# Weight stores on ScalarE's queue, token norms from the transposed input, and attention biases and maxima as product rows

## The chip, the cores and the metric

The kernel runs on one core of a Trainium2 chip. The metric is the device time of one execution in microseconds. Before the change it is 1830.58 us, the median of 3 runs (1828.81 to 1836.41).

## What is computed

One layer of a streaming encoder. 2048 prompt tokens and 128 sample tokens (8 sequences of 16), each 1024 wide, are normalised and projected to the columns of three groups of heads; the gated outputs of the groups go through one output projection.

```python
h = rms_norm(x, norm_g) @ w_in
fox_cols, rwkv_cols, mem_cols = jnp.split(h, [FOX_COLS, FOX_COLS + RWKV_COLS], axis=-1)
q, k, v, logf, g_f = fox_prep(fox_cols, fox_q_g, fox_k_g, fox_b_f)
...
s = s + jnp.transpose(cq, (0, 2, 1))[..., :, None] - jnp.transpose(ck, (0, 2, 1))[..., None, :]
mask = kpos[None, :] <= qpos[:, None]
s = jnp.where(mask, s, jnp.finfo(jnp.float32).min)
p = jax.nn.softmax(s, axis=-1)
...
o = jnp.concatenate([o_f.astype(x.dtype) * jax.nn.silu(g_f),
                     o_r * jax.nn.silu(g_r),
                     o_m * jax.nn.silu(g_m)], axis=-1)
y = x + o @ w_out
```

`fox` is causal attention with 6 heads of 64 whose logits carry a bias: `c`, the running sum of the log forget gates, is added for the query and subtracted for the key. `rwkv` is a recurrent mixer with 6 heads, `mem` is attention with 4 heads over 256 memory tokens. All is in float32.

## The kernel before, in words

**Products in two parts.** A float32 matrix is held as a high part, rounded to the type fp32r, and a low part, the rest. A product is then three fp32r products: high by high, high by low, low by high.

**First part (the pools of `p1`).** The tokens are taken in four passes of 512. The first pass has the 128 sample tokens as well, so 640. `prep_x` (L218 on) prepares a pass: it loads the tokens as rows, squares them on ScalarE with a running sum per row (L238 in the first pass, L243 later), takes the power -1/2 on GpSimd, and turns the factors into a row for all partitions (`pb`, copied to `rb`, L252). It then loads the transposed tokens in 8 tiles of 128 rows (`xraw`, L267), scales them on VectorE (L65 is the helper's line), and splits them into `xk` (high by ScalarE, L270, low by GpSimd or VectorE). In the first pass this is done for 256 columns and then for 384.

`wd_load` (L172 on) brings weights: in the first pass it loads the raw ones (L196), makes the high part on ScalarE (L197) and the low part on GpSimd, and stores both parts in DRAM (`w_d`, L200); the later passes load the stored parts (L192). `proj_d` makes columns by tokens (`pjd`), `wide` tokens by columns (`pjt`). Results of `wide` go through the buffer `qk` (two of them, L705) to DRAM (L713). In the last pass `forget` works out the running sums and stores the negated ones as rows `nc_d`.

**Second part (`p2`).** The fox heads go in 3 pairs by 4 query blocks of 512, the memory heads in 2 pairs by 4 blocks. Keys are loaded per 512 tokens (`tok`, L980), turned by TensorE (`pt`, L983) and split into `K1` and `K2`; queries into `Q1` and `Q2`. `fox_max` makes the scores once with the queries on the partitions (`pm`), adds the key bias (`nb`, a copy of the bias row in all 128 partitions, L1011), and takes the row maximum, both in one VectorE instruction (L1063). `negate` and `rows_` turn the negated maxima to a row: a transpose (`pr`, L1082), a copy to `m8` (L1084), a store to DRAM (L1086) and two loads into row 64 of `Q2` (L1088). `scores` then makes the scores again with the keys on the partitions (`pS`) in two products. The first has the query's high and low parts stacked against the key's high part twice, the second the query's high part with the row of maxima against the key's low part with a row of ones. The exponential (L1117) adds the key's bias per partition and gives `P`, which ScalarE and GpSimd split into `Ph` (L1120) and `Pl`; `values` makes the outputs `po`. The sample tokens' attention (`sample`) and the output projection (`py`, in pieces) are mixed in between.

**What sets the order.** The code emits all instructions, and `_arrange` at its end orders each engine's instructions anew. It simulates the engines and the DMA queue with costs written in `_Op`, several times with other ranks (`_TRIES`, `_AGAIN`), and keeps the order with the least total. Every DMA of the kernel before is issued by SP, so all share one queue, which takes them in order: a transfer that must wait for its data holds those behind it.

Of the kernel before, what the change touches and what calls it, by code (L numbers as in the profile page):

```python
# [9 lines left out]
F32 = mybir.dt.float32  # L10
# [7 lines left out]
KC = 8  # L18
# [33 lines left out]
def kernel(ctx: ExitStack, tc: tile.TileContext, I: dict, O: dict):  # L52
# [62 lines left out]
    nc_d = dt("nc_d", [6, TP])  # L115
# [7 lines left out]
    with ExitStack() as p1:  # L123
# [48 lines left out]
        def wd_load(*parts, src="w_in"):  # L172
# [14 lines left out]
            for j, k0 in enumerate(range(0, KC, 4)):  # L187
# [5 lines left out]
                else:  # L193
# [5 lines left out]
                    if key in split:  # L199
                        SY.dma_start(split[key][128 * j:128 * j + 128], flat.bitcast(F32))  # L200
# [17 lines left out]
        def prep_x(tok0, n, xtok, xT, gcol, tiles=None, between=lambda: None):  # L218
# [9 lines left out]
            for t0, t1 in ((0, 2), (2, 5)) if first else ((0, nt),):  # L228
                c0, c1 = 128 * t0, 128 * t1
                for t in range(t0, t1):  # L230
                    if first:
                        if t % 2 == 0:
                            two = rv.tile([128, 2, D], F32, tag="gm" if t < 4 else "su", name="xt", bufs=2 if t < 4 else 1)
                        xt = two[:, t % 2]
                    r0 = TP if t == 4 else tok0 + 128 * t
                    if first:
                        SY.dma_start(xt, xtok[r0:r0 + 128, :])
                        S.activation(xt, xt, AF.Square, accum_out=ssq[:, 0, t:t + 1])  # L238
                    else:
# [4 lines left out]
                if not first:  # L244
                    tt(V, ssq[:, 0, :nt], ssq[:, 0, :nt], ssq[:, 1, :nt], A_)
                rsqrt_small(rsq[:, t0:t1], ssq[:, 0, t0:t1], t1 - t0, 1.0 / D, EPS)
# [6 lines left out]
                for k in range(KC):  # L253
                    if not t0:
                        xk.append(tiles[k] if tiles else xs_.tile([128, 2, 640], F32R, tag="xk", name="xk", bufs=XKB))
                        if not first:
                            raw = xs_.tile([128, 512], F32, tag="xraw", name="xraw", bufs=3)
                        elif k < 6:
                            if k % 3 == 0:
                                three = ws.tile([128, 2, 4, 256], F32, tag="hl", name="xraw").rearrange("p x a b -> p (x a b)")  # L260
                            raw = three[:, 640 * (k % 3):640 * (k % 3) + 640]
                        else:
                            raw = rv.tile([128, 640], F32, tag=("bk", "bt")[k - 6], name="xraw")
                        raws.append(raw)
                    raw, hl = raws[k], xk[k]
                    for a, m, r0 in spans(tok0, c0, c1 - c0):
                        SY.dma_start(raw[:, c0 + a:c0 + a + m], xT[128 * k:128 * (k + 1), r0:r0 + m])  # L267
# [520 lines left out]
        def forget():  # L788
# [137 lines left out]
    with ExitStack() as p2:  # L926
# [21 lines left out]
        S.copy(negT, negm[:, 2, :])  # L948
        idb = c2t("idb", [128, 128], BF16)
# [20 lines left out]
        def split_keys(k1, k2, src, n):  # L970
            src = src[:, :n]
            S.copy(k1[0:64, :n], src)
            S.copy(k1[64:128, :n], src)  # L973
            tt(V, k2[0:64, :n], src, k1[0:64, :n].bitcast(F32), SUB)
            G.memset(k2[64:65, :n].bitcast(F32), 1.0)
# [20 lines left out]
        def fox_keys(U, hp):  # L996
# [4 lines left out]
            def block(g0):  # L1001
                if not g0:
                    U["nb"] = kp.tile([128, 2, TP], F32, tag="nb", name="nb")
                gs = slice(g0, g0 + 512)
                pt = turned_in(k_d[gs, cs], 512)
                k1 = [kp.tile([128, 512], F32R, tag="K1", name="K1", bufs=2 * NKB) for _ in range(2)]
                k2 = [kp.tile([65, 512], F32R, tag="K2", name="K2", bufs=2 * NKB) for _ in range(2)]
                for h in range(2):
                    split_keys(k1[h], k2[h], pt[64 * h:64 * h + 64], 512)
                for h in range(2):  # L1010
                    SY.dma_start(U["nb"][:, h, gs], nc_d[2 * hp + h, gs].partition_broadcast(128))  # L1011
# [7 lines left out]
        def mem_keys(U, hp):  # L1019
            cs = slice(128 * hp, 128 * hp + 128)  # L1020

            def step():
# [3 lines left out]
                k1 = [m[:, 256 * h:256 * h + 256] for h in range(2)]  # L1026
                k2 = [m[0:65, 512 + 256 * h:768 + 256 * h] for h in range(2)]
# [6 lines left out]
        def queries(U, q, qsrc, qb, hp, fox):  # L1034

            s_ = "" if fox else "m"

            def load():
                pt = turned_in(qsrc, 512)
                if fox:  # L1040
                    q["Q1"] = [wk.tile([128, 512], F32R, tag=f"Q1{h}", name=f"Q1{h}") for h in range(2)]
                    q["Q2"] = [wk.tile([65, 512], F32R, tag=f"Q2{h}", name=f"Q2{h}") for h in range(2)]
                else:
                    m = big("Qm", F32R)
                    q["Q1"] = [m[:, 512 * h:512 * h + 512] for h in range(2)]
                    q["Q2"] = [m[0:65, 512 * h:512 * h + 512] for h in (2, 3)]
# [5 lines left out]
                q["mx"] = wk.tile([128, 2, 4], F32, tag="mx" + s_, name="mx", bufs=1 + fox)  # L1052

            def fox_max(h, t, c0, nk):
# [4 lines left out]
                if end:  # L1059
                    mm(pm[:, n - 128:n], idb, negb, start=False)  # L1060
                jk = wk.tile([128, 512], BF16, tag="jk", name="jk", bufs=1)
                m_ = q["mx"][:, h, t:t + 1]
                V.tensor_tensor_reduce(out=jk[:, :n], in0=pm[:, :n], in1=U["nb"][:, h, c0:c0 + n], scale=1.0,  # L1063
                                       scalar=-3.0e38 if c0 == 0 else m_, op0=A_, op1=MAX, accum_out=m_)
# [947 lines left out]
```

## Time and profile before

| | before |
|---|---|
| median of 3 runs | 1830.58 us (1828.81 to 1836.41) |
| the profiled execution, its own time | 1832.25 us |
| its span | 1830.5 us |
| TensorE busy | 1718.1 us, 94% |
| mean granted clock of TensorE | 0.971 |
| VectorE, ScalarE, GpSimd busy | 934.0, 872.3, 782.4 us |
| DMA | 301.34 MB, mean 165 GB/s |

In the profile PE is TensorE's matmuls and PEld its weight loads, which overlap them; DVE is VectorE, ACT ScalarE, POOL GpSimd, SP SyncE, and SPq its sequencer that issues DMAs. A row of the groups reads: line, engine, operation, output<-inputs, shapes, count | busy us, mean ns of one | idle time of the engine just before them, and what ended most of it. A row of the timeline begins with its start and its length in us, and a bracket gives the idle time before it and what ended that. A row of the waits reads: engine, what waited, what it waited for: us in total, times, the longest. Many lines go through helpers (L59 is every product, L62, L65 and L68 the elementwise ones), so the names tell them apart.

### The profile page before, as it was taken

The numbers are of one execution on the slowest core, as the hardware profiler recorded it, in microseconds if no ns is written. First come the engines' busy times: TensorE is split into PE (matmuls) and PEld (weight loads), VectorE is DVE, ScalarE is ACT, GpSimd is POOL, SyncE is SP. The second block draws the span as 40 slices with busy tenths as digits, with TensorE's granted clock in tenths as the row PEclk, the third lists the DMA queues.
The fourth block names the chain that finished last, engine by engine and source line by source line (L and its number), as shares of the span: only waits on it lengthen the run. The fifth ranks groups of instructions, "written<-read, shape, count | busy, mean of one in ns | idle before, by whom it ended". The sixth has DMA issues, their size and how long they took to land. (4 is left out here: it accounts for less than half of the span.)

```text
span 1830.5 us, 42049 instructions
## 1 busy us (share of the span) xinstructions
PE 1718.1 (94%) x16743; PEld 1370.1 (75%) x16743; DVE 934.0 (51%) x2325; ACT 872.3 (48%) x1727; POOL 782.4 (43%) x790
## 2 busy tenths in 40 slices
PE   4989999999999999999999998799899898999998
PEld 3989989788887788887888886567576555667776
DVE  6543354474444564364754543867346654485213
ACT  5424342533243424325232433687787565986351
POOL 5565252232322243031322241377586364866562
PEclk9999999999999999999999998799999898999999
DMA  7665463644445645456454454434647645262432
GB/s 230 246 219 200 144 205 125 202 163 151 168 157 168 223 128 190 138 174 195 155 170 134 134 177 123 156 121 143 203 138 248 195 141 173 87 209 87 163 111 89
DMA packets 213273, 301.34 MB, mean 165 GB/s; under 512 B 57444, under 2 KB 162454, under 8 KB 197206
## 3 DMA queue, kind: packets, MB, share of 16 engines
q1 hardware_dynamic: 213078, 298.66, 49.6%
q8 instruction: 131, 2.15, 0.5%
q14 instruction: 64, 0.52, 0.1%
HBM read 211.47 MB, written 87.12 MB: 163 GB/s over the span
## 5 line engine op out<-in xcount | busy, mean ns | idle before, releaser
L59 PE MATMUL pjd<-xk,w 128*128 128x512 f32 (+4 forms) x2280 | 520.1, 373 | 14.6 <-DVE xk L62 6.7
L59 PEld LDWEIGHTS pjd<-xk,w 128*128 128x128 f32 (+1 forms) x2280 | 381.9, 190 | 79.1 <-issue 10.8
L62 POOL TENSOR_TENSOR Pl<-P,Ph 128x512 fp32r<-128x512 f32 (+3 forms) x272 | 315.5, 1174 | 150.5 <-ACT Ph L1120 127.6
L59 PE MATMUL pjt<-w,xk 128*128 128x256 f32 x2040 | 292.6, 291 | 4.4 <-ACT qk L705 4.4
L59 PEld LDWEIGHTS pjt<-w,xk 128*128 128x128 f32 x2040 | 263.9, 191 | 17.9 <-issue 7.7
L59 PE MATMUL py<-W,oh 128*128 128x512 f32 x816 | 236.2, 402 | 2.3 <-DVE rb L1162 1.6
L1117 ACT ACTIVATE P<-pS,NB 128x512 f32<-128x512 f32 x240 | 147.9, 623 | 85.6 <-PE pS L59 57.5
L59 PEld LDWEIGHTS py<-W,oh 128*128 128x128 f32 x816 | 150.5, 190 | 38.3 <-DVE rb L1162 2.1
L59 PE MATMUL pS<-Q,K 128*128 128x512 f32 (+2 forms) x480 | 155.5, 392 | 8.3 <-ACT P L1117 8.0
L1120 ACT CAST Ph<-P 128x512 fp32r<-128x512 f32 (+3 forms) x272 | 150.1, 564 | 7.7 <-PE po L59 2.9
L59 PE MATMUL po<-Ph,vt 128*65 128x512 f32 x480 | 151.3, 373 | 1.2 <-ACT ob L1143 0.7
L59 PEld LDWEIGHTS pS<-Q,K 128*128 128x128 f32 (+1 forms) x480 | 87.4, 195 | 40.5 <-ACT P L1117 24.7
L62 DVE TENSOR_TENSOR xo<-py,xo 128x512 f32<-128x512 f32 x68 | 46.5, 686 | 133.1 <-PE py L59 127.8
L59 PE MATMUL pm<-K,Q 128*128 128x512 f32 (+2 forms) x240 | 95.8, 411 | 19.5 <-DVE Q L62 13.1
L62 POOL TENSOR_TENSOR nr<-nr,mhalf 128x8 f32<-128x8 f32 (+2 forms) x43 | 61.2, 1424 | 122.9 <-DVE nr L68 106.4
L1063 DVE CUSTOM_DVE_ANT_0 jk<-pm,nb,mx 128x512 bf16<-128x512 f32 (+3 forms) x144 | 93.2, 647 | 33.7 <-PE pm L59 25.1
L62 POOL TENSOR_TENSOR w<-wraw,w 128x1024 fp32r<-128x1024 f32 (+1 forms) x34 | 79.6, 2343 | 46.6 <-ACT w L197 42.2
L59 PE MATMUL po<-Pl,vt 128*65 128x512 f32 x240 | 88.3, 369 | 1.8 <-POOL Pl L62 1.7
L705 ACT COPY qk<-pjt 128x512 f32<-128x512 f32 (+1 forms) x47 | 26.5, 563 | 131.0 <-PE pjt L59 104.3
L59 PEld LDWEIGHTS po<-Ph,vt 128*65 128x65 f32 x480 | 64.0, 139 | 27.3 <-ACT Ph L1120 2.4
L59 PEld LDWEIGHTS pm<-K,Q 128*128 128x128 f32 x240 | 47.1, 198 | 44.7 <-DVE mx L1063 18.2
L62 POOL TENSOR_TENSOR oh<-ot,oh 128x384 fp32r<-128x384 f32 (+2 forms) x38 | 44.9, 1183 | 74.3 <-ACT oh L1323 39.5
(392 smaller groups left out, 2820.9 us busy)
## 6 DMA issues: line engine op xcount, KB each, us to landing
w<-w_d SPq DMA_DIRECT2D x84, 1024.0 KB
w_d<-w SPq DMA_DIRECT2D x28, 1024.0 KB
y_d<-xo SPq DMA_DIRECT2D x21, 512.0 KB
wraw<-in_w_in SPq DMA_DIRECT2D x36, 256.0 KB
xo<-in_x SPq DMA_DIRECT2D x17, 512.0 KB
xo<-y_d SPq DMA_DIRECT2D x17, 512.0 KB
xt<-in_x SPq DMA_DIRECT2D x24, 256.0 KB
xraw<-in_xT SPq DMA_DIRECT2D x24, 256.0 KB
```

Of the source, the lines that this page charges most:

```text
L59: PE.matmul(out, lhsT, rhs, start=start, stop=stop, skip_group_check=True)
L62: e.tensor_tensor(out=out, in0=a, in1=b, op=op)
L705: S.copy(o_, out)
L1063: V.tensor_tensor_reduce(out=jk[:, :n], in0=pm[:, :n], in1=U["nb"][:, h, c0:c0 + n], scale=1.0, scalar=-3.0e38 if c0 == 0 else m_, op0=A_, ...
L1117: S.activation(P_[:, c0:], pS[:, c0:], AF.Exp, bias=NB[:, qb, 2 * hp + h, kt:kt + 1] if fox else 0.0)
L1120: S.copy(Ph[:, c0:], P_[:, c0:])
```

## The change

It has four parts and a change to the planner.

- The stores of the split weights are issued by ScalarE instead of SP, so they have a queue of their own.
- In the first pass the tokens' row loads go. The transposed tiles are loaded earlier, ScalarE squares them into a scratch tile, and products with a column of ones (`pq`, one column each, 40 in all) sum them over the partitions.
- The key bias of the maxima becomes two rows (high and low part) of `K1`, against rows of ones in `Q1`; the broadcast `nb` and the fused add and maximum go, and a plain maximum per 512 keys stays. `K1` now has 67 rows with the high part, and `K2` has the high part over the low part.
- The row of negated maxima is made by four fp32r products with an identity (`pr`, 33 rows of 128) and two copies of a row into `Q1`; the store and the two loads go.
- The planner charges DMAs to the engine that issues them, with a wire for each queue, and takes six rounds instead of five.

```diff
-nc_d = dt("nc_d", [6, TP])
+nc_d = dt("nc_d", [12, TP])
...
                     if key in split:
-                        SY.dma_start(split[key][128 * j:128 * j + 128], flat.bitcast(F32))
+                        S.dma_start(split[key][128 * j:128 * j + 128], flat.bitcast(F32))
...
+                if first:
+                    m = c1 - c0
+                    sqs = [rv.tile([128, 8, 256], F32, tag="gm", name="xsq", bufs=2)] if not t0 else [
+                        rv.tile([128, 5, 384], F32, tag="gm", name="xsq", bufs=2), rv.tile([128, 3, 384], F32, tag="su", name="xsq2")]
+                    pq = ps.tile([128, 512], F32, tag="ra", name="pq")
+                    for k in range(KC):
...
+                        for a, w, r0 in spans(tok0, c0, m):
+                            SY.dma_start(raws[k][:, c0 + a:c0 + a + w], xT[128 * k:128 * (k + 1), r0:r0 + w])
+                        sq = sqs[k // 5 if t0 else 0][:, k % 5 if t0 else k, :]
+                        S.activation(sq, raws[k][:, c0:c1], AF.Square)
+                        for t in range(t1 - t0):
+                            mm(pq[:, t:t + 1], sq[:, 128 * t:128 * t + 128], one1, start=k + t == 0, stop=k == KC - 1)
+                    rsqrt_small(rsq[:, t0:t1], pq[:, 0:t1 - t0], t1 - t0, 1.0 / D, EPS)
...
-            nr = sm.tile([96, 128], F32, tag="w4", name="nr", bufs=1)
-            V.tensor_copy(nr, pn[0:96, 0:128])
-            SY.dma_start(nc_d.rearrange("h (t p) -> (h t) p", p=128), nr)
+            nr = sm.tile([96, 2, 128], F32R, tag="w4", name="nr", bufs=1)
+            S.copy(nr[:, 0], pn[0:96, 0:128])
+            tt(V, nr[:, 1], pn[0:96, 0:128], nr[:, 0].bitcast(F32), SUB)
+            for a in range(2):
+                SY.dma_start(nc_d[6 * a:6 * a + 6].rearrange("h (t p) -> (h t) p", p=128), nr[:, a].bitcast(F32))
...
             S.copy(k1[0:64, :n], src)
-            S.copy(k1[64:128, :n], src)
-            tt(V, k2[0:64, :n], src, k1[0:64, :n].bitcast(F32), SUB)
-            G.memset(k2[64:65, :n].bitcast(F32), 1.0)
+            S.copy(k2[0:64, :n], src)
+            tt(V, k2[64:128, :n], src, k1[0:64, :n].bitcast(F32), SUB)
+            G.memset(k1[64:65, :n].bitcast(F32), 1.0)
...
-                for h in range(2):
-                    SY.dma_start(U["nb"][:, h, gs], nc_d[2 * hp + h, gs].partition_broadcast(128))
+                    SY.dma_start(k1[h][65:67, :].bitcast(F32), nc_d[2 * hp + h:2 * hp + h + 7:6, gs])
...
-                    S.copy(q["Q2"][h][0:64], src)
-                    tt(V, q["Q1"][h][64:128], src, q["Q1"][h][0:64].bitcast(F32), SUB)
+                    S.copy(q["Q2"][h][64:128], src)
+                    tt(V, q["Q2"][h][0:64], src, q["Q1"][h][0:64].bitcast(F32), SUB)
+                    if fox:
+                        G.memset(q["Q1"][h][64:67].bitcast(F32), 1.0)
...
-                V.tensor_tensor_reduce(out=jk[:, :n], in0=pm[:, :n], in1=U["nb"][:, h, c0:c0 + n], scale=1.0,
-                                       scalar=-3.0e38 if c0 == 0 else m_, op0=A_, op1=MAX, accum_out=m_)
+                V.tensor_reduce(out=q["mx"][:, h, t, c0 // 512:c0 // 512 + 1], in_=pm[:, :n], op=MAX, axis=AX.X)
...
-                PE.transpose(pr[0:8, 0:128], q["mx"].rearrange("p h t -> p (h t)"), ident)
-                m8 = wk.tile([8, 128], F32R, tag="m8", name="m8")
-                S.copy(m8, pr[0:8, 0:128])
-                md = dt("md", [8, 128], bufs=4)
-                SY.dma_start(md, m8.bitcast(F32))
+                for t in range(4):
+                    mm(pr[0:33, 128 * t:128 * t + 128], q["mr"][:, t, :], idr)
                 for h in range(2):
-                    SY.dma_start(q["Q2"][h][64:65, :].bitcast(F32), md[4 * h:4 * h + 4].rearrange("(o t) c -> o (t c)", o=1))
+                    S.copy(q["Q1"][h][64:65], pr[32 * h:32 * h + 1])
...
-                mm(pS[:, c0:], k1, q["Q1"][h][:, c0:], stop=False)
+                mm(pS[:, c0:], k2, q["Q2"][h][:, c0:], stop=False)
                 diag = fox and kt >= 4 * qb
-                mm(pS[:, c0:], k2, q["Q2"][h][:, c0:], start=False, stop=not diag)
+                mm(pS[:, c0:], k1[0:65], q["Q1"][h][0:65, c0:], start=False, stop=not diag)
...
-_AGAIN = 5
+_AGAIN = 6
...
-            rank = [(1 - _SHIFT) * a + _SHIFT * b for a, b in zip(rank, late)]
+            rank = [(1 - _SHIFT) * a + _SHIFT * (b + c) / 2 for a, b, c in zip(rank, start, late)]
```

The order shifts all through the program. Three places matter here. The first is ScalarE at the program's start. There `xt` are the tokens as rows with their sums `ssq`, `xsq` the squares of the transposed tiles, `rb` the row of factors, `xk` the high parts and `w` those of the weights. Before:

```order
L197 CAST w<-wraw 128x280 x2
L238 ACTIVATE xt,ssq<-xt 128x1024 x5
L252 COPY rb<-pb 128x256
L270 CAST xk<-xraw 128x256
L252 COPY rb<-pb 128x256
L270 CAST xk<-xraw 128x256
```

And with the change:

```order
L247 ACTIVATE xsq<-xraw 128x256 x8
L247 ACTIVATE xsq<-xraw 128x384 x3
L265 COPY rb<-pb 128x256
L247 ACTIVATE xsq<-xraw 128x384 x2
L275 CAST xk<-xraw 128x256 x2
L247 ACTIVATE xsq_247<-xraw 128x384
L275 CAST xk<-xraw 128x256 x4
L247 ACTIVATE xsq_247<-xraw 128x384
L197 CAST w<-wraw 128x280 x2
```

The squares of the second half now stand between the copies of the first, and the first weights' high parts come after them.

The second place is ScalarE a little later in the first pass, with the change, where the stores `w_d<-w` stand among the high parts of weights (L197) and the evictions of `pjt` into `qk`:

```order
L710 COPY qk<-pjt 128x512
L692 ACTIVATE nsq<-qk 128x512
L710 COPY qk<-pjt 128x512
L692 ACTIVATE nsq<-qk 128x512
L197 CAST w<-wraw 128x1024 x2
L710 COPY qk<-pjt 128x256
L200 DMA w_d<-w 128x2048 x2
L692 ACTIVATE nsq<-qk 128x256
L197 CAST w<-wraw 128x1024 x2
L710 COPY qk<-pjt 128x512 x2
```

Before, no DMA stands in this engine's row; the stores stood in SP's, between the raw weights and the stores of `qk`.

The third place is SP's queue at the entry into the attention: `tok` and `vtok` are the keys, queries and values of a block, `nb` the broadcast bias, `K` the rows of bias. Before:

```order
L980 DMA tok<-k_d 128x4x128
L988 DMA vtok<-v_d 128x4x128
L980 DMA tok<-q_d 128x4x128
L941 DMA negm<-in_negm 128x384
L1011 DMA nb<-nc_d 128x512 x6
L754 DMA mg_d<-gth 128x512
L1011 DMA nb<-nc_d 128x512
L980 DMA tok<-k_d 128x4x128
L1011 DMA nb<-nc_d 128x512
L647 DMA o_d<-bv 128x512
```

And with the change:

```order
L995 DMA tok<-q_d 128x4x128
L948 DMA negm<-in_negm 128x384
L759 DMA mg_d<-gth 128x512
L930 DMA out_rs_p<-sstp 64x6x64
L652 DMA o_d<-bv 128x512
L1023 DMA K_14040<-nc_d 2x512
L995 DMA tok<-k_d 128x4x128
L1003 DMA vtok<-v_d 128x4x128
L995 DMA tok<-q_d 128x4x128
L1023 DMA K_14041<-nc_d 2x512
```

The second block's keys, values and queries follow the first block's after a handful of rows, without the eight broadcasts ahead of them.

More of the change, by code (lines that the diff above doesn't have):

```diff
@@ L229, in prep_x @@
                 c0, c1 = 128 * t0, 128 * t1
[L230 to L239, printed above, removed]
+                if first:
[4 more added lines that the diff above has]
+                    for k in range(KC):
+                        if not t0:
+                            if k < 6:
+                                if k % 3 == 0:
+                                    three = ws.tile([128, 2, 4, 256], F32, tag="hl", name="xraw").rearrange("p x a b -> p (x a b)")
+                                raws.append(three[:, 640 * (k % 3):640 * (k % 3) + 640])
+                            else:
+                                raws.append(rv.tile([128, 640], F32, tag=("bk", "bt")[k - 6], name="xraw"))
+                        for a, w, r0 in spans(tok0, c0, m):
[5 more added lines that the diff above has]
+                    rsqrt_small(rsq[:, t0:t1], pq[:, 0:t1 - t0], t1 - t0, 1.0 / D, EPS)
+                else:
+                    for t in range(t0, t1):
+                        r0 = tok0 + 128 * t
                         for j in range(2):
@@ L243, in prep_x @@
                             S.activation(xt, xt, AF.Square, accum_out=ssq[:, j, t:t + 1])
-                if not first:
                     tt(V, ssq[:, 0, :nt], ssq[:, 0, :nt], ssq[:, 1, :nt], A_)
-                rsqrt_small(rsq[:, t0:t1], ssq[:, 0, t0:t1], t1 - t0, 1.0 / D, EPS)
+                    rsqrt_small(rsq[:, t0:t1], ssq[:, 0, t0:t1], t1 - t0, 1.0 / D, EPS)
                 pb = pj.tile([128, 512], F32, tag="pj", name="pb")
@@ L256, in prep_x @@
                         if not first:
[L257 to L264, printed above, removed]
+                            raws.append(xs_.tile([128, 512], F32, tag="xraw", name="xraw", bufs=3))
+                            SY.dma_start(raws[k][:, :n], xT[128 * k:128 * (k + 1), tok0:tok0 + n])
                     raw, hl = raws[k], xk[k]
-                    for a, m, r0 in spans(tok0, c0, c1 - c0):
-                        SY.dma_start(raw[:, c0 + a:c0 + a + m], xT[128 * k:128 * (k + 1), r0:r0 + m])
                     for r_, o, a, b in cuts:
@@ L948 @@
         S.copy(negT, negm[:, 2, :])
+        idr = c2t("idr", [128, 128], F32R)
+        S.copy(idr, ident)
+        turnm = [c2t(f"turnm{j}", [128, 4, 33], F32R) for j in range(4)]
+        for x in turnm:
+            G.memset(x.bitcast(F32), 0.0)
+        taken = [0, 0]
         idb = c2t("idb", [128, 128], BF16)
@@ L1025, in step @@
                 pt = turned_in(mk_d[:, cs], 256)
-                k1 = [m[:, 256 * h:256 * h + 256] for h in range(2)]
-                k2 = [m[0:65, 512 + 256 * h:768 + 256 * h] for h in range(2)]
+                k1 = [m[0:65, 256 * h:256 * h + 256] for h in range(2)]
+                k2 = [m[:, 512 + 256 * h:768 + 256 * h] for h in range(2)]
                 for h in range(2):
@@ L1036, in queries @@
             s_ = "" if fox else "m"
+            q["mr"] = turnm[2 * (not fox) + taken[fox] % 2]
+            taken[fox] += 1
             def load():
@@ L1553, in __init__ @@
             return
+        self.wire = 0
         psum = any("PSUM" in space(a) for a in aps)
         scalar = n > 1 and any(k == 1 for k in sizes)
-        if eng == "SP":
+        if "DMA" in kind:
             size = 4 * list(outs[0].ap)[0][1] * _free(list(outs[0].ap))
@@ L1776, in _schedule @@
     ready, end, done, start = [0] * count, [0] * count, [False] * count, [0] * count
-    released, alive, pooled, wire, base, order, why = {}, set(), {}, 0, 0, [], [[] for _ in nodes]
+    released, alive, pooled, wire, base, order, why = {}, set(), {}, {}, 0, [], [[] for _ in nodes]
     cand = {e: [x for x in range(count) if not need[x] and of[x] == e] for e in free}
@@ L1837, in _schedule @@
         c = cost[nodes[x][0]]
-        if e == "SP":
+        if e == "SP" or e == "Activation" and c.wire:
             free[e] = s + c.own
-            wire = max(wire, s + c.own + 300) + c.wire
-            end[x] = wire + c.time
+            a, b = max(wire.get(e, 0), s + c.own + 300), max([0] + [t for q, t in wire.items() if q != e])
+            wire[e] = a + c.wire + min(max(0, b - a), c.wire)
+            end[x] = wire[e] + c.time
         elif e == "PE":
```

38 lines of the change are left out of this document (20 added, 18 removed).

## The prediction

> **What bounds the kernel now.** I read the page first (engine shares, the slices), then the windows, then the timelines of the stretches in which TensorE stands still.
>
> ```profile
> span 1830.5 us, 42049 instructions
> PE 1718.1 (94%) x16743; PEld 1370.1 (75%) x16743; DVE 934.0 (51%) x2325; ACT 872.3 (48%) x1727; POOL 782.4 (43%) x790
> ...
> PE   4989999999999999999999998799899898999998
> ...
> PEclk9999999999999999999999998799999898999999
> ```
>
> TensorE is the bound: busy 1718.1 us, so 112.4 us are idle, and they lie at the start, past the middle (slices 25 and 26) and in the last third. In the same places the granted clock sinks. A change that leaves the products alone can only win back idle time and time at a low clock. Four stretches, with PE busy in the first busy column and the clock in the column before the DMA share:
>
> ```profile
> 0.00:50.00 50.00, 22.96 (x104) 18.60 (x105) 30.79 (x72) 25.98 (x57) 23.51 (x33) 0.90 0.78 243
> 100.00:150.00 50.00, 43.21 (x334) 41.63 (x333) 22.66 (x59) 15.02 (x28) 29.54 (x25) 0.97 0.58 195
> ...
> 1130.00:1200.00 70.00, 53.05 (x234) 35.38 (x232) 52.95 (x124) 45.46 (x89) 23.65 (x27) 0.76 0.54 170
> 1200.00:1700.00 500.00, 467.77 (x2722) 321.38 (x2721) 291.47 (x708) 364.30 (x690) 321.83 (x302) 0.96 0.49 161
> ```
>
> Idle: 27.0, 6.8, 17.0 and 32.2 us, 83 of the 112. Lost to the clock: 5.0, 1.5, 16.8 and 20 us (share missing times length). The change touches all four.
>
> **The start: norms from the transposed tokens.**
>
> ```profile
> 0.74 2.10 SPq L196 DMA_DIRECT2D wraw<-in_w_in  x4
> ...
> 4.65 1.28 ACT L197 ACT_TABLE_LOAD   x1 [4.65 <-DMA wraw<-in_w_in]
> ...
> 9.81 1.06 ACT L238 ACTIVATE xt<-xt 128x1024 f32<-128x1024 f32 x1 [3.12 <-DMA xt<-in_x]
> ...
> 14.93 0.19 ACT L238 ACTIVATION_READ_ACCUMULATOR xt<-xt 128x1 f32 x1
> ...
> 16.16 2.50 PE L59 MATMUL pb<-ident,rsq 128*128 128x128 f32 x10 [16.16 <-POOL rsq L62]
> ...
> 17.83 5.06 DVE L65 SCALAR_TENSOR_TENSOR xraw<-xraw,vec,rb 128x256 f32<-128x256 f32 x9 [2.44 <-ACT rb L252]
> ...
> 18.74 0.41 ACT L270 CAST xk<-xraw 128x256 fp32r<-128x256 f32 x1 [0.95 <-DVE xraw L65]
> ...
> 30.60 0.55 DVE L62 TENSOR_TENSOR xk<-xraw,xk 128x384 fp32r<-128x384 f32 x1
> ...
> 35.30 0.28 DVE L65 SCALAR_TENSOR_TENSOR centre<-bones,ident 128x128 f32<-128x128 f32 x1
> ...
> 36.37 1.05 DVE L62 TENSOR_TENSOR xk<-xraw,xk 128x384 fp32r<-128x384 f32 x1 [0.79 <-ACT xk L270]
> ...
> 41.79 18.48 PE L59 MATMUL pjd<-xk,w 128*128 128x256 f32 x110 [1.89 <-DVE fl L62]
> ```
>
> Before, five loads of 512 KB must land and be squared; scaling starts 2.71 us after the last read-out ends (15.12 to 17.83). Then VectorE scales and splits until 37.42, and full-width products start at 41.79. Now eight loads of 128 KB are first in SP's queue. At 0.525 us an issue (2.10 for 4) the last is issued at 4.9; at the 1.8 us from the weights' last issue (2.84) to their first use after that wait (4.65), it is there at 6.7. The first has landed at 3.1 by the same lag, the table load of 1.28 follows, and ScalarE squares eight tiles of 256 at about 0.41 us (the copy of that size), done near 7.7; the column products add some 0.4 (an estimate from small products elsewhere), so scaling starts near 10.8, 7 us earlier. The second half waits for more: 22 further issues lie ahead of its last load, which lands at 18 to 20; squares, column products and the 2.71 put its scaling at 22 to 24. From there VectorE has 8 x (0.56 + 0.28) + 4 x 0.55 = 9 us, to 31 to 33 instead of 37.4. Gain 4 to 6; I take **-5**, bounds -9 (the whole 7 and clock) to -1 (ScalarE's second squares, which stand between the copies, come late). The squares cost 8 x 0.41 + 8 x 0.5 = 7.3 us (0.5 for 384 is an estimate from the 0.41) against 5 x (1.06 + 0.19) = 6.2, beside loads. The 40 column products lie in idle time.
>
> **The first pass: stores of split weights on ScalarE's queue.**
>
> ```profile
> ACT qk L705 <- DMA mq_d<-qk: 8.1, 3, 5.6
> ...
> PE pjt L59 <- ACT qk L705: 4.2, 1, 4.2
> ```
>
> ```profile
> L200 SPq DMA_DIRECT2D w_d<-w x30: 377/503/1362, 28.0 to 296.7; - x30
> ```
>
> ```profile
> L62 POOL TENSOR_TENSOR w<-wraw,w 128x1024 fp32r<-128x1024 f32 x32 | 78.1, 2444 | 44.0 <-ACT w L197 39.6 <-issue 4.2
> ```
>
> From 110 to 140 us ScalarE waits 8.1 us for stores of 128 KB that stand behind 1 MB weight stores in the one queue; TensorE waits for ScalarE behind that. A second queue lets the small ones past. What can come back is the 6.8 idle and 1.5 of clock in 100 to 150: I take **-5**, bounds -9 and 0. The issues cost ScalarE 30 x 0.503 = 15 us, 58 of 150 busy there, hidden. No row shows a DMA issued by ScalarE; the price is SP's. The danger is not the issue but its wait, since each store needs GpSimd's low half (2.444 us); that is a rival below. By the Trainium skill (DMA: Bandwidth & Descriptors, "Issuing engines are not separate DMA queues") all issuers' transfers run on the same 16 engines and a second issuer saves only issue time; by that rule this term would be 0. No run here shows two issuers yet.
>
> **The entry into the attention.**
>
> ```profile
> 1127.92 4.39 SPq L1011 DMA_DIRECT2D nb<-nc_d  x6
> ...
> 1139.51 0.52 SPq L980 DMA_DIRECT2D tok<-q_d  x1
> ```
>
> ```profile
> 1144.53 1.11 PE L983 MATMUL pt<-ident,tok 128*128 128x128 f32 x4 [0.26 <-DMA tok<-q_d]
> ...
> 1151.05 0.80 PE L59 MATMUL pm<-K,Q 128*128 128x512 f32 x1 [5.40 <-DVE Q L62]
> ```
>
> ```profile
> 1158.37 0.69 ACT L1117 ACTIVATE P<-pS,NB 128x512 f32<-128x512 f32 x1 [3.97 <-PE pS L59]
> ```
>
> Eight broadcasts of 256 KB stand ahead of the second block's queries, which are issued at 1139.51 and land at 1144.5. Now rows of 4 KB take their place: 4.39 us of issue go for six, up to 5.9 for eight (I take 5), and 2 MB of traffic (an estimated 2 us of the 5 to landing). The products of the maxima also need only the high halves, so VectorE's split (0.69) leaves their way. The maxima reach the scores by four products and two copies instead of a store and two loads. That is 7 to 10 us for the first exponential. What is late next is ScalarE's own row of copies: 20 of 0.58. TensorE gains part of its idle 17.0 and some clock. I take **-9**, bounds -14 and -3. The Trainium skill (TensorE: Matmul & The Clock Gate, "What's actually happening") has the clock halve after an idle window of about 3.4 us; the gaps of 5.4 at a clock of 0.76 agree, and by it the gain here would go to 15 or more if no such gap were left.
>
> **The steady attention.** VectorE gains, ScalarE and GpSimd lose.
>
> ```profile
> L1063 DVE CUSTOM_DVE_ANT_0 jk<-pm,nb,mx 128x512 bf16<-128x512 f32 x90 | 67.2, 747 | 22.9 <-PE pm L59 18.4
> L1063 DVE CUSTOM_DVE_ANT_0 jk<-pm,nb 128x512 bf16<-128x512 f32 x78 | 53.6, 687 | 18.4 <-PE pm L59 14.5
> ...
> L1070 DVE TENSOR_REDUCE mx<-pm 128x2 f32<-128x512 f32 x32 | 21.3, 686 | 7.3 <-PE pm L59 7.2
> L1063 DVE DVE_READ_ACCUMULATOR2_ANT mx<- 128x1 f32 x240 | 19.6, 82 | 0.0
> ...
> L975 POOL MEMSET K<- 1x512 f32 x24 | 12.1, 520 | 1.0
> L1139 ACT COPY rs<-po 1x512 f32<-1x512 f32 x20 | 11.6, 580 | 18.3 <-PE po L59 18.0
> ```
>
> ```profile
> L1084 ACT CAST m<-pr x20: 238/255/256, 1144.3 to 1706.2; 8x128 fp32r<-8x128 f32 x20
> ```
>
> ```profile
> PE pS L59 <- ACT P L1117: 10.6, 11, 2.9
> PE pt3b L1263 <- DVE sD L68: 8.3, 6, 3.1
> PE pm L59 <- DVE mx L1063: 5.5, 10, 1.0
> ```
>
> - VectorE: 168 reductions of 512 cost 67.2 + 53.6, and all read-outs 19.6; plain ones cost 168 x 0.686 = 115.2. That is 25 us less, little of it on the path: of the 13.8 us that TensorE waits for VectorE in 1200 to 1700 I take a third, -5.
> - ScalarE: 40 rows of 512 at 0.580 for 20 of 0.255: +18.1 us, on an engine busy 364 of 500, and in front of exponentials that TensorE waits for (10.6). A fifth shows: +4.
> - GpSimd: 24 more fills like the one of 0.520: +12.5 us, cover 178 of 500 us idle: 0; without it as ScalarE's.
> - TensorE: 80 narrow products for 20 transposes. Products of 128 columns follow each other in about 0.06 us (below): at most +4 us, I take +2; the wider reuse of keys and queries keeps the number of products.
>
> ```profile
> 1231.31 0.28 PE L59 MATMUL po<-Ph,vt 128*65 128x128 f32 x2
> 1231.43 0.22 PE L59 MATMUL po<-Pl,vt 128*65 128x128 f32 x1
> ```
>
> Sum here +1, bounds -14 (VectorE's waits whole) and +12 (two thirds of ScalarE's). The order of the whole program is worked out anew; I give that 0, with 4 us either way.
>
> **Sum.** -5 - 5 - 9 + 1 = -18. The profiled execution took 1832.25 us (span 1830.5 and 1.75 around it), so 1814; the runs' median, 1830.58, is 1.7 lower, which puts the forecast at **1812.6**. About 0.5%, 9.2 us, is what a measurement can tell from no change: faster is under 1821.4, slower over 1839.7.
>
> **Rivals.**
> 1. *The second queue gives nothing and the start's second half is late* (the rule above): the first pass 0, the start -1, the entry -6, the attention +1: -6, so 1825, no change. For it: TensorE's named waits in the first pass are few. Against it: the 5.6 us wait for a store of 128 KB. Chance 0.17.
> 2. *Stores stall ScalarE.* A store placed among copies holds every later eviction until GpSimd's low half is done. Half a low half each, 28 x 1.22 = 34 us, in the path gives 1830.6 - 14 + 34 - 1 = 1850, slower. It decides once the holds that reach TensorE exceed 13 us beyond that to 0.5%, about 23 us. Against it: three output buffers and the waits of GpSimd, mostly for ScalarE (39.6), which show it free. Chance 0.08.
> 3. *The attention opens up.* With VectorE freed, the reductions' waits and the clock's 20 us go together: -14 there and -12 at the entry make 1830.6 - 36 = 1795. Against it: ScalarE's added rows. Chance 0.15.
>
> The forecast itself gets 0.60. Faster is 0.60 + 0.15 = 0.75, the same 0.17, slower 0.08. Its own bounds, combined rather than all at one end, are 1800 to 1823; leaving out rival 2 and half of rival 3 gives **1797 to 1829**.
>
> **What would show it.** Right: the first wide product near 35 us instead of 41.8; no wait for a store in 110 to 140; the first exponential 7 to 10 us earlier relative to the end of the first part; reductions at 0.69 us without read-outs. Wrong: ScalarE idle before its weight stores for tens of us; the scores' wait for exponentials growing from 10.6 to over 25; the first pass as long as before.

## The result and the profile after

The changed kernel takes 1839.70 us, the median of 14 runs (1834.94 to 1851.41), beside 1830.55 us for the kernel before on the same chips (14 runs). The ratio is 1.0058, 95% interval 1.0043 to 1.0072: about 0.6% slower, 27 us above the forecast and outside its range. Its profiled execution took 1841.82 us.

From the page of the changed kernel, the span, TensorE's shares and its granted clock by slices:

```profile
span 1840.0 us, 41935 instructions
...
PE 1757.5 (96%) x16883; PEld 1398.7 (76%) x16883; DVE 933.9 (51%) x2102; ACT 893.9 (49%) x1755; POOL 794.0 (43%) x818
...
PEclk8999999999999999999998999799999698999999
```

TensorE's idle time fell from 112.4 to 82.5 us, which is the kind of gain that was forecast. Its busy time rose from 1718.1 to 1757.5. So 30 us less of waiting stand against 39 us more of work. The slices of low clock are fewer past the middle and deeper in the last third; the mean is 0.965 instead of 0.971.

The same four stretches as before (PE busy first, the clock before the DMA share):

```profile
0.00:50.00 50.00, 37.04 (x164) 32.87 (x164) 23.33 (x56) 25.68 (x57) 22.13 (x31) 0.86 0.64 185
100.00:150.00 50.00, 45.40 (x649) 42.75 (x649) 26.77 (x56) 15.70 (x32) 26.18 (x24) 0.97 0.50 163
1130.00:1200.00 70.00, 58.71 (x318) 40.00 (x318) 45.80 (x88) 50.09 (x96) 34.37 (x45) 0.83 0.46 143
1200.00:1700.00 500.00, 482.02 (x2753) 328.10 (x2752) 281.21 (x523) 378.25 (x706) 325.52 (x319) 0.95 0.46 151
```

All four are busier than before, by 14.1, 2.2, 5.7 and 14.3 us. Busier is not faster: in the first stretch the column products alone take more than the added 14 us.

The start, TensorE's timeline (a row that groups products shows the shape of its first one):

```profile
3.28 6.99 PE L59 MATMUL pq<-one,xsq 128*128 128x1 f32 x32 [3.28 <-ACT xsq L247]
...
14.16 7.68 PE L59 MATMUL pq<-one,xsq 128*128 128x1 f32 x36
...
46.40 3.82 PE L59 MATMUL pjd<-xk,w 128*128 128x256 f32 x24
...
51.63 4.54 PE L59 MATMUL pjd<-xk,w 128*128 128x384 f32 x25 [1.12 <-DVE fl L62]
```

A column product is not small: each is two instructions that load 128x128 weights for one column; 32 such instructions take 6.99 us, 0.22 us apiece. The full-width products that started at 41.79 before now start at 46.40, 4.6 us later: 24 run there, and the others from 51.63 on.

The end of the first part is the copy `sstp<-pst`, the start of the attention's exponentials the first `P<-pS`. ScalarE's timeline before, for the first of the two:

```profile
1129.92 0.47 ACT L922 COPY sstp<-pst 64x384 f32<-64x384 f32 x1 [2.78 <-PE pst L920]
```

And after, both:

```profile
1143.60 0.47 ACT L929 COPY sstp<-pst 64x384 f32<-64x384 f32 x1 [2.07 <-PE pst L927]
...
1163.23 0.69 ACT L1134 ACTIVATE P<-pS,NB 128x512 f32<-128x512 f32 x1 [0.63 <-PE pS L59]
```

Three differences make up the whole: the first part ends 13.7 us later, the first exponential follows after 19.6 instead of 28.5 us (-8.8), and from there to the end it takes 676.8 instead of 672.1 us (+4.6 before rounding). That is +9.5 of span.

The attention's own rows, from the groups of the changed kernel with shapes kept apart, then from its waits:

```profile
L1078 DVE TENSOR_REDUCE mx<-pm 128x1 f32<-128x512 f32 x168 | 111.7, 686 | 53.2 <-PE pm L59 52.5
```

```profile
PE pm L59 <- DVE mx L1078: 8.4, 12, 1.6
...
PE pS L59 <- ACT P L1134: 2.7, 7, 1.2
...
PE pS L59 <- ACT Q L1105: 1.4, 2, 0.8
```

The plain reductions take 0.686 us, as taken from the memory heads' row; the scores' wait for exponentials shrank from 10.6 to 2.7 instead of growing. The last row is new: the scores wait for ScalarE's copies of the maxima's row.

### The profile page after: what moved, and what is told of

Same layout as the page of the kernel before. It is cut to its first block, busy times and chain, and to the rows that moved or that the text cites. A ratio compares the mean times of both kernels' runs of the same rounds, so it can differ in the third digit from the quotient of the medians.

```text
span 1840.0 us, 41935 instructions
## 1 busy us (share of the span) xinstructions
PE 1757.5 (96%) x16883; PEld 1398.7 (76%) x16883; DVE 933.9 (51%) x2102; ACT 893.9 (49%) x1755; POOL 794.0 (43%) x818
## 4 chain that ended last, share of the span: by engine, by line
PE 73%; DVE 6%; ACT 5%; DMA 4%; issue 3%; POOL 2%; SPq 1%; ACTq 0%; DVEq 0%; POOLq 0%
PE pjd L59 18%; PE pjt L59 11%; PE py L59 10%; PE po L59 8%; PE pS L59 6%; PE pm L59 3%; PE sc L59 2%; PE sy L59 2%; PE pa L59 1%; PE pz L59 1%; PE gr L59 1%; DVE mx L1078 1%; PE spr L59 1%; ACT P L1134 1%; PE gw L59 1%
## 5 line engine op out<-in xcount | busy, mean ns | idle before, releaser
L59 PE MATMUL pjd<-xk,w 128*128 128x512 f32 (+5 forms) x2280 | 533.3, 376 | 14.6 <-ACT xk L275 4.9
L59 PE MATMUL pjt<-w,xk 128*128 128x256 f32 x2040 | 285.1, 290 | 0.0
L59 PE MATMUL py<-W,oh 128*128 128x512 f32 x816 | 243.2, 402 | 1.4 <-DVE rb L1179 0.7
L1078 DVE TENSOR_REDUCE mx<-pm 128x1 f32<-128x512 f32 (+2 forms) x240 | 139.9, 605 | 69.9 <-PE pm L59 68.4
L1137 ACT CAST Ph<-P 128x512 fp32r<-128x512 f32 (+3 forms) x272 | 150.9, 564 | 18.1 <-PE po L59 13.7
L59 PEld LDWEIGHTS pS<-Q,K 128*128 128x128 f32 (+1 forms) x480 | 87.6, 197 | 39.6 <-ACT P L1134 17.4
L59 PE MATMUL pm<-K,Q 67*128 67x512 f32 (+2 forms) x240 | 99.4, 432 | 10.0 <-DVE mx L1078 8.4
L59 PEld LDWEIGHTS pm<-K,Q 67*128 67x128 f32 x240 | 50.1, 211 | 30.4 <-DVE mx L1078 18.2
```

The lines of the kernel that those rows point to most:

```text
L59: PE.matmul(out, lhsT, rhs, start=start, stop=stop, skip_group_check=True)
L1078: V.tensor_reduce(out=q["mx"][:, h, t, c0 // 512:c0 // 512 + 1], in_=pm[:, :n], op=MAX, axis=AX.X)
L1137: S.copy(Ph[:, c0:], P_[:, c0:])
```

## The experiments

Ratios are to the kernel before, run on the same chip each time; medians of different experiments are from different chips. "The first part" is the time to `sstp<-pst`, "the rest" what is left of the span, both from the one profiled execution.

### One part at a time

Theory 1 held that the start had failed. `planner_only` has the rule for ranks, the six rounds and the DMA costs alone; `norms_only` and `attention_only` add one part to it, `all_but_norms` is the changed kernel with `prep_x` as before.

```diff
-_AGAIN = 5
+_AGAIN = 6
...
-            rank = [(1 - _SHIFT) * a + _SHIFT * b for a, b in zip(rank, late)]
+            rank = [(1 - _SHIFT) * a + _SHIFT * (b + c) / 2 for a, b, c in zip(rank, start, late)]
```

> The kernel before with only the planner's changes (costs of DMAs, six rounds, ranks from starts and latest starts). Theory 1: within 3 us of before. Rival A: slower by 6 us or more, with the first part as long as in the changed kernel.

> The kernel before with the planner's changes and, of the change, only the norms of the first pass from the transposed tokens. Theory 1 (the start is what failed: 40 column products at about 0.43 us each, and the second half's row of factors held behind a constant): first wide product near 51 us as in the changed kernel, and slower than before by 6 to 12 us, 1836 to 1843. Rival A (the new order of the first part costs the time, whichever part is in): about as much slower as the planner alone. Rival B (the stores on ScalarE's queue cost it): within 3 us of before.

> The changed kernel with the norms of the first pass as before. Theory 1: the start is as before (first wide product near 42), and the kernel is 8 to 14 us faster than the changed one, 1825 to 1832 beside 1839.7. Rivals A and B: the first part stays some 13 us longer, so within 4 us of the changed kernel.

> The kernel before with the planner's changes and only the attention's biases and maxima by products. Theory 1: faster than before by 2 to 6 us, nearly all of it at the entry into the attention (first exponential 7 to 10 us sooner after the end of the first part, the rest of the attention 2 to 6 us longer). My prediction had -8 for this part. Rival A: the gain at the entry is lost in the first part, no faster than before.

| | median us | ratio, interval | first part |
|---|---|---|---|
| planner_only | 1850.68 | 1.0125 (1.0103 to 1.0146) | 1158.9 |
| norms_only | 1854.04 | 1.0146 (1.0113 to 1.0180) | 1156.1 |
| all_but_norms | 1843.25 | 1.0081 (1.0060 to 1.0102) | 1149.2 |
| attention_only | 1839.31 | 1.0045 (1.0024 to 1.0066) | 1133.9 |

Theory 1 fell. The planner's change alone, without one instruction more or less, costs 1.25%, some 22 us, more than the whole change. The late start does go with the norms: the first full-width products stand at 46.7 us in `norms_only` and near 42 (two of them at 39.7) in `all_but_norms`. The times do not follow it: the norms cost 3 us where they are added to the planner's change and gain 4 where they complete the change, so no sign can be read from them. ScalarE's row in `planner_only`, for the end of the first part:

```profile
1158.91 0.47 ACT L922 COPY sstp<-pst 64x384 f32<-64x384 f32 x1 [7.20 <-PE pst L920]
```

This is 29 us later than in the kernel before, with the same instructions in another order.

### How much the order alone is worth

The planner makes 15 orders (18 in the changed kernel) and takes the one with the least total in its own reckoning. These kernels take the second, third or fourth best. `after_old_rule` was to have the changed kernel's instructions with the rounds and ranks of before; its one edit sets the rounds to five, and the rule for ranks is still the changed one.

```diff
-    _, start = min(found, key=lambda x: x[0])
+    _, start = sorted(found, key=lambda x: x[0])[1]
```

> The kernel before, instruction for instruction, in the second best of the 15 orders that its planner tried (its own total is 1764.8 us beside 1762.6 for the best). Theory 2 (the order alone decides by 10 to 20 us, and the planner's total does not tell which is good): 1835 to 1855, several us slower than before, though the planner has the two 0.1% apart. Rival C (only the changed rule for the ranks gives bad orders): within 4 us of 1829.

> The kernel before in the third best of its planner's 15 orders (1765.9 us by the planner). Theory 2 (the order the kernel before has is a fortunate one among its own): 1838 to 1855. If its order is an ordinary one and the second best an unlucky one: 1825 to 1836.

> The kernel before in the fourth best of its planner's 15 orders (1766.1 us by the planner). As for the third: 1838 to 1855 if the order of the kernel before is a fortunate one, 1825 to 1836 if not.

> The changed kernel in the second best of its planner's 18 orders (1702.3 us by the planner beside 1700.6). Theory 2: anywhere from 1825 to 1855, over 4 us away from the 1839.7 of the changed kernel. Rival C: within 4 us of it.

> The changed kernel in the third best of its planner's 18 orders (1713.7 us by the planner). The four best orders of the kernel before stand at ratios 1, 1.011, 1.0075 and 1.0006, mean 1.005. If the parts give what I predicted (1%), orders of the changed kernel scatter around 0.995: 1810 to 1832. If they give a third of it or less, around 1.003: 1826 to 1846, as its first two orders did (1.0058 and 1.0017).

> The changed kernel in the fourth best of its planner's 18 orders (1714.8 us by the planner). As for the third: 1810 to 1832 if the parts give 1%, 1826 to 1846 if a third of it or less.

> The changed kernel with the rounds and the rule for ranks as before (5 rounds, latest starts alone); all else as changed. Rival C: 1810 to 1822, the parts then give what I predicted. Theory 2: the parts give some of it, but the order adds its own 10 us either way: 1825 to 1850 as likely as below.

| order | best | second | third | fourth | mean |
|---|---|---|---|---|---|
| before | 1 | 1.0110 | 1.0075 | 1.0006 | 1.0048 |
| changed | 1.0058 | 1.0017 | 1.0061 | 1.0097 | 1.0058 |
| before, first part us | 1129.9 | 1129.6 | 1139.7 | 1131.0 | 1132.6 |
| changed, first part us | 1143.6 | 1147.4 | 1140.2 | 1145.4 | 1144.1 |
| before, rest us | 700.6 | 711.8 | 701.4 | 703.4 | 704.3 |
| changed, rest us | 696.4 | 692.3 | 697.9 | 695.4 | 695.5 |

The intervals are about 0.2% to 0.4% either way. `after_old_rule` stands at 1.0028 (1.0009 to 1.0048). Its instructions ran in the order of `after_third` on every engine (save pairs that start within some 0.02 us of each other), so the two are one program on two chips, and its ratio came out as 1.0061 and as 1.0028: differences of 0.3% between rows of different chips are not told apart from none. Its profiled executions have first parts of 1140.2 and 1140.7 us and rests of 697.9 and 689.0, so one execution places the first part well here and the rest only to some 9 us. Whether the rule for ranks gives worse orders was not tested alone; the orders of before and of `attn_old` below, made by the old rule, include slow ones too.

Orders of the kernel before that its planner holds equal within 0.2% differ by 1.1% on the chip, and the order that it had is the best of its four, with the fourth not told apart from it. The means are 0.1% apart, where 1% was forecast. By the scatter of the four orders on each side that difference is known to some 0.7% either way (an estimate): a gain as forecast is unlikely, a small one or a small loss is not excluded. The rest is 8.8 us shorter on average, and the first part 11.6 us longer. The two trade against each other by the order as well: `planner_only`, with the attention unchanged, ends its first part at 1158.9 and needs 688.1 for the rest, and `attention_only` has 1133.9 and 703.6. So neither stretch can be judged alone.

### The stores on a second queue, in a fixed order

`stores_pinned` is the kernel before with ScalarE issuing the stores. The planner still takes them for SP's, so the other instructions keep their order on every engine. `after_stores_sp` is the reverse: the changed kernel with the stores back on SP at the places planned for ScalarE.

```diff
-                        SY.dma_start(split[key][128 * j:128 * j + 128], flat.bitcast(F32))
+                        S.dma_start(split[key][128 * j:128 * j + 128], flat.bitcast(F32))
...
-    eng = [str(i.engine).split(".")[-1] for i in ins]
+    eng = ["SP" if "DMA" in type(i).__name__ else str(i.engine).split(".")[-1] for i in ins]
...
```

> The kernel before with only the stores of the split weights on ScalarE's queue, and the order of every engine kept as before: the planner still takes those stores for SP's, so each stands in ScalarE's row where its start was planned. This is my term of -5 (bounds -9 to 0) without any new order. If the term is right: 1820 to 1826. If the second queue gives nothing (rival 1): within 2 us of before. If stores hold ScalarE (rival 2): slower by 5 us or more, with ScalarE idle before them.

> The changed kernel with the stores of the split weights issued by SP again, each at the place in SP's row where the planner had them on ScalarE; every other row unchanged. If a second queue costs something by itself, as the pinned test on the kernel before showed (+10): faster than the changed kernel by 3 to 10 us. If that test showed only stores in unplanned places: slower than the changed kernel by 3 to 10 us here, for the same reason the other way about. If the queue is without effect: within 3 us.

`stores_pinned` took 1842.96 us, 1.0054 (1.0029 to 1.0079): some 10 us slower. ScalarE's waits for GpSimd's low halves and for the stores `mq_d`, then its timeline at the worst of them, then TensorE's:

```profile
ACT qk L705 <- POOL w L62: 7.2, 2, 4.0
ACT xt L243 <- POOL w L62: 3.2, 2, 2.1
ACT w L197 <- POOL w L62: 1.2, 1, 1.2
...
ACT qk L705 <- DMA mq_d<-qk: 7.2, 3, 4.7
```

```profile
111.03 0.39 ACTq L200 DMA_DIRECT2D w_d<-w  x1
111.46 0.59 ACT L705 COPY qk<-pjt 128x512 f32<-128x512 f32 x1 [3.98 <-POOL w L62]
```

```profile
112.10 9.07 PE L59 MATMUL pjt<-w,xk 128*128 128x256 f32 x57 [4.26 <-ACT qk L705]
```

The store waits for the low half, the eviction waits behind the store, and TensorE waits 4.26 us for the eviction. This is rival 2, with 11.6 us of holds instead of the 34 that it was given; the kernel before has no such wait. TensorE's 4.26 us are the part of the 10 that a row shows. The waits for `mq_d`, from which the prediction took its gain, stay at 7.2 us of 8.1 although the weight stores now have their own queue: most of that wait did not come from sharing one. In the changed kernel, whose planner counts the stores as ScalarE's, no such hold is left either, and taking its stores back to SP gave 1839.21 us, 1.0038 (1.0014 to 1.0062): beside 1.0058 that is not told apart from no effect. Neither test shows a gain from the second queue. That agrees with the Trainium skill (DMA: Bandwidth & Descriptors, "Issuing engines are not separate DMA queues"), by which a second issuer saves issue time alone.

### The start in order

`after_start_hand` moves 14 groups of instructions in the changed kernel's order, all in the first 50 us, by a table of times; two of its lines:

```diff
+_MOVE = (("Activation", "xk_223", 34000, 34500, 31080), ("Activation", "reset", 21000, 22000, 31100),
...
+         ("Pool", "w_464", 28000, 28500, 34000), ("Pool", "w_471", 30500, 31000, 34010),
```

> The changed kernel with its order changed by hand in the first 50 us alone: on ScalarE, VectorE and GpSimd the copies of constants, the low halves of the second weights and one square of the next pass stand behind the second half's factors, scalings and splits; all else keeps its order. Theory 1 (the late start is a real loss of its own): the first products with 128 columns of weights 4 to 8 us earlier and the kernel as much faster than the changed one, 1832 to 1836. If the rest of the order swallows it: first wide product earlier, time within 3 us.

It took 1843.33 us, 1.0070 (1.0046 to 1.0094), no faster than the changed kernel. TensorE's timeline and, below it, ScalarE's:

```profile
38.87 4.51 PE L59 MATMUL pjd<-xk,w 128*128 128x256 f32 x22 [1.82 <-POOL w L62]
47.91 0.48 PE L315 MATMUL pf<-ident,fsb 6*128 6x6 f32 x3 [4.53 <-ACT fsb L312]
50.94 5.39 PE L59 MATMUL pjd<-xk,w 128*128 128x384 f32 x16 [2.54 <-DVE fl L62]
```

```profile
46.32 1.04 ACT L197 CAST w<-wraw 128x1024 fp32r<-128x1024 f32 x1 [8.13 <-DMA wraw<-in_w_in]
```

The full-width products start at 38.87 (two stand at 36.65), but the second batch of them stands at 50.94, where it was, since the next raw weights land at 46.3. So earlier splits alone do not help while the weights come late. In the changed kernel SP waits for the weights' buffer (SP's waits from 20 to 52 us):

```profile
SPq L196 <- POOL w L62: 9.8, 1, 9.8
```

In the kernel before the longest such wait of that stretch is 2.2 us. In `after_start_hand` the moves themselves hold the weights:

```profile
SPq L256 <- ACT reset L781: 6.4, 1, 6.4
SPq L196 <- POOL w L62: 4.5, 2, 3.9
```

A token load ahead of the weights in SP's row waits 6.4 us for the constant's copy, and the weights' buffer waits for the low half, which were both moved back. What a start would give with early splits and early weights was not tried.

### The attention alone, and with the first part's order kept

`attn_old` and `attn_old_second` are the kernel before with the attention's part alone, under its own planner, in the two best orders.

> The kernel before with only the attention's biases and maxima by products, under the planner of before (no change of ranks, rounds or costs). If the entry's -9 and the steady +1 are right, its orders scatter around 1.005 - 0.0044, that is 1.000: 1820 to 1840, mean of the two 1831. If the added products and copies take the entry's gain back: mean of the two about 1839.

> The same in the second best order of that planner (1741.1 us by the planner beside 1739.2). As for attn_old: mean of the two 1831 if entry and steady attention are as predicted, about 1839 if the entry's gain is given back.

They gave 1833.46 us, 1.0020 (1.0003 to 1.0038), and 1839.09 us, 1.0055 (1.0035 to 1.0074). The rest was 688.4 and 689.5 us, shorter than in any order of before; the first part was 1146.4 and 1148.5, longer than in any, though all that changed in it is the making of the bias rows. By the trade just seen, this could be the order's or the edit's. So the last two kernels hold the first part's order fixed: its instructions keep the times that the planner gave them in the kernel before (a table, `kept`), and the second part's times, from the orders above, move up by the difference.

```diff
+    rank = [kept[m[0]] if m[0] < len(kept) else start[x] - shift for x, m in enumerate(runs[0])]
```

> The kernel before with only the attention's biases and maxima by products; the first part's instructions keep the planned times of the kernel before (a table), the second part those that its own planner gave it in its best order, moved up by the 9.9 us by which that planner ended the first part later. If the longer first part was only the order's: first part 1130 as in before, the rest 688 to 692 beside 700.6, so 1818 to 1823, a ratio of 0.993 to 0.997, faster than both kernels. If the attention's shorter stretch needs the later start (loads and low halves that run ahead into the first part): the rest about 700, and within 4 us of before.

> The same with the second part in its planner's second best order, moved up by 15.6 us. As for attn_kept: 1818 to 1824 if the longer first part was only the order's, within 4 us of before if not.

They took 1819.91 us, 0.9935 (0.9914 to 0.9957), and 1822.33 us, 0.9946 (0.9928 to 0.9964): faster than both kernels. The page of `attn_kept`, its windows for the attention, and ScalarE's timeline:

```profile
span 1820.7 us, 41762 instructions
...
PE 1733.2 (95%) x16803; PEld 1378.6 (76%) x16803; DVE 923.0 (51%) x2102; ACT 888.8 (49%) x1749; POOL 794.1 (44%) x818
```

```profile
1130.00:1200.00 70.00, 61.77 (x271) 41.10 (x271) 49.71 (x91) 55.70 (x107) 34.52 (x42) 0.78 0.47 147
1200.00:1700.00 500.00, 482.03 (x2783) 331.19 (x2782) 285.85 (x521) 372.44 (x698) 325.61 (x317) 0.96 0.46 152
```

```profile
1130.75 0.47 ACT L924 COPY sstp<-pst 64x384 f32<-64x384 f32 x1 [2.37 <-PE pst L922]
...
1150.25 0.69 ACT L1129 ACTIVATE P<-pS,NB 128x512 f32<-128x512 f32 x1 [1.23 <-PE pS L59]
```

The first part is as before (1130.75 beside 1129.92), the entry is 19.5 us long instead of 28.5, and from the first exponential to the end it takes 670.5 instead of 672.1. In `attn_kept_second` these are 1132.4, 19.4 and 675.5, in a profiled execution of 1829.10 us, the longest of its twelve. The longer first part of `attn_old` thus belonged to the order that came with the change, not to the attention's part.

## Why the prediction was wrong

- **The order, given 0 with 4 either way: this step failed.** It is the largest term. The same instructions lie between 1829 and 1851 us (`planner_only`, 1.0125), and the kernel before stands at the fast end, 0.5% below the mean of its four best orders. For the attention's part it is shown that the new order cost more than the part gained: 1.0020 and 1.0055 against 0.9935 and 0.9946, 16 and 20 us. In the sum for the changed kernel, the first part's +13.7 us stands where -10 was forecast; how much of that is the order's and how much the norms' and the stores' own is not separated.
- **The start, -5: wrong in its working and not a gain.** The column products were put at 0.4 us, an estimate from other small products, and into idle time. They take 17.4 us of TensorE and keep it busy until 10.3 and from 14.2 to 21.8, ahead of the factors of each half. The first half's scaling began at 14.8 instead of 10.8 (17.8 before). Scaling of the second half was expected at 22 to 24; it began at 29.2. The last 2.4 us of that are a constant's copy that ScalarE had ahead of the row of factors, whose products had ended at 26.4 (ScalarE's timeline, then VectorE's):

```profile
28.59 0.30 ACT L781 CAST reset<-craw 128x128 bf16<-128x128 f32 x1 [6.44 <-DMA craw<-in_reset]
28.80 0.53 ACT L265 COPY rb<-pb 128x256 f32<-128x256 f32 x2
```

```profile
29.19 3.47 DVE L65 SCALAR_TENSOR_TENSOR xraw<-xraw,vec,rb 128x256 f32<-128x256 f32 x8 [5.47 <-ACT rb L265]
```

  Moving that away gained nothing, for the raw weights came late too, in that test by its own moves. I had followed the tokens and not the weights' buffers.
- **The stores, -5: the mechanism was wrong, and the gain did not come.** That a second queue lets the small stores past is not what the runs show: in a fixed order 7.2 of the 8.1 us of waiting stayed. In the changed kernel ScalarE still waits once for a store of `qk` there (4.1 us), though no wait of TensorE between 110 and 140 us follows from it, and TensorE's idle time in 100 to 150 fell from 6.8 to 4.6 us; over the whole program ScalarE's named waits for stores of `qk` went from 15.3 to 15.9 us. In a fixed order the stores cost 10 us, with rival 2's holds in the trace; where the planner knows of them, nothing that can be told from zero.
- **The entry, -9: right in size.** With the first part's order kept, 28.5 us became 19.5, by -8.95, and TensorE's gaps of 4.14 and 5.40 us are gone; the longest is 2.77. The mark moves with the order too (`planner_only`, with the attention as before, has 13.7 us there), so that the gain is the edit's rests on a first part that ends at the same time; the second part's order is a new one. The clock in 1130 to 1200 rose only from 0.76 to 0.78, so the 15 or more that was worked out from the Trainium skill (TensorE: Matmul & The Clock Gate, "What's actually happening") for a stretch without long gaps did not come. Two rows of windows bear on that, the first of the kernel before, the second of `attn_kept`:

```profile
1130.00:1150.00 20.00, 10.37 (x35) 6.27 (x33) 12.35 (x31) 10.11 (x20) 0.49 (x2) 0.50 0.84 265
```

```profile
1150.00:1164.00 14.00, 14.00 (x56) 10.06 (x55) 11.31 (x20) 11.64 (x25) 7.40 (x10) 0.50 0.57 179
```

  Before, the clock was at half from 1130 on, ahead of both gaps, which end at 1136.16 and 1151.05; so the gap of 5.4 us, which the prediction took as agreeing, is not what brought it down. In `attn_kept` it stayed at half through 14 us in which the profile has TensorE busy without a break. What sets it here stays open.
- **The steady attention, +1: right within its bounds.** It measured -1.7 in the profiled execution of `attn_kept` and +3.4 in that of `attn_kept_second`; with some 9 us between two executions of one program, that it lies so near +1 is luck. The 168 full reductions cost VectorE 111.7 us in the changed kernel, where the fused ones stood with 120.8 and all read-outs with 19.6, yet TensorE's wait for them between 1200 and 1700 us stayed at 5.6 there after 5.5 (2.2 in `attn_kept`); the ScalarE rows cost TensorE 1.4 us of new waits in the changed kernel. On TensorE the 80 narrow products take 8.9 us instead of 5.5 for the transposes, and the 240 products of maxima 99.4 instead of 95.8.
- **The idle time itself.** I said that TensorE can only win back idle time and clock. It did win back 30 us of idle time, and the time still rose. But the change does not leave the products alone: the column products take 17.4 us, the narrow ones 3.4 and the maxima 3.6 more than before, 24 of the 39 us of added work, and the clock's share lost (span times one less the mean clock) went from 53 to 64 us.

Rival 1 had the two right ideas (no gain from the queue, a late second half) but a price of -6; none of the rivals had the order.

It stays open why the planner's better totals go with a longer first part, and whether the norms or the stores would show anything in a first part of otherwise kept order: that was not tried.

## What to carry to other kernels

Where a planner orders the instructions anew after each edit, an edit is compared with an order as well as with a kernel: time a few orders of equal total on both sides, or hold the order fixed outside the edit, before a difference under 1% is put down to the edit. A gain in one stretch is safe only if the order elsewhere is kept; here the same edit gave +0.2% to +0.6% or -0.6%, and one program gave ratios 0.3% apart on two chips. And a product with one column is as dear as its weight load: 80 such instructions took 17.4 us here, their 80 loads 17.5.

## What the runs showed of the hardware

- A float32 product of 128x128 weights with one column took two instructions of 0.22 us each in a row, 17.4 us for 40, at a granted clock of 1.00; TensorE was as long busy with their weight loads, 17.5 us. A Square that feeds two or three of them took 0.4 to 0.5 us.
- Issuing a store took ScalarE 0.391 us in the median, in the changed kernel, against 0.503 for SP before; and a store that waited for its data held ScalarE's next eviction for up to 4.0 us in `stores_pinned`.

```profile
L200 ACTq DMA_DIRECT2D w_d<-w x30: 326/391/399, 20.7 to 293.7; - x30
```

- One program's instructions in other orders differed by up to 1.25% in time (1.0000 to 1.0125 over five orders), while TensorE's busy time ranged from 1718 to 1743 us. Busy time times mean granted clock (0.971 to 0.962) stays within 0.5%, 1668 to 1677 us, so most of the longer busy time is a lower clock: the order moves the work's own length and not only the waiting.
- The granted clock stood at half while the profile has TensorE busy without a break: 0.50 from 1150 to 1164 us in `attn_kept`, busy 14.00 of 14.00 us.
